# SSD exponents from log time steps, elementwise work of two stages from GpSimd to VectorE, and modulation in 256-column parts begun in the SSD stage

## The chip, the cores and the metric

The kernel runs on one core of one Trainium2 chip. TensorE (PE) multiplies matrices, VectorE (DVE), ScalarE (ACT) and GpSimd (POOL) work elementwise, SyncE (SP) issues most of the loads. The metric is the device time of one execution in microseconds: the median of three runs, 1510.19 us.

## The reference

Two layers of a diffusion backbone run over 256 context and 256 latent tokens of width 1024, with a modulation (shift, scale, gate) from a small matrix product per layer. Only what the change touches is shown. Layer 0's SSD heads are computed in chunks of 128 tokens, forward and backward:

```python
mod_l = (jax.nn.silu(c) @ ada_w[layer] + ada_b[layer])[:, None, :]       # 6 x 1024 columns
# SSD, one chunk, one direction: xi = x * dt, ai = dt * neg_a
acum = jnp.cumsum(ai, axis=-1)
seg = jnp.where(lower, acum[..., :, None] - acum[..., None, :], -jnp.inf)
scores = jnp.einsum('bgin,bgjn->bgij', ci, bi)[:, :, None] * jnp.exp(seg)
y = jnp.einsum('bgrij,bgrjp->bgrip', scores, xi)
y = y + jnp.einsum('bgin,bgrpn->bgrip', ci, h) * jnp.exp(acum)[..., None]
xw = xi * jnp.exp(acum[..., -1:] - acum)[..., None]
h = h * jnp.exp(acum[..., -1])[..., None, None] + jnp.einsum('bgjn,bgrjp->bgrpn', bi, xw)
# GLA: o from decayed q, k and v, then
o = rmsnorm(o, gla_norm_w).reshape(bn, t, GLA_VAL) * jax.nn.silu(r)
```

Then come an output projection and a squared-ReLU MLP; layer 1 has HGRN2 and S5 heads in place of SSD and GLA, and an MLP of its own.

## The kernel before, in words

Everything is in one unrolled program of 24495 instructions. Its stages follow one another: norm and the first modulation parts (0 to 45 us of the trace), layer 0's input projection with convolutions (to 155), the SSD stage (to about 313), the GLA stage (to 498), output projection, MLP 0 (600 to 975), then layer 1. The order of the instructions on each engine is made by a planner that simulates the program with a cost model of its own and takes ready work by the order of the source; engines run their queues in that order.

Weights come as 512 KB tiles into a ring of four (`wraw`, L214). Each is split on chip: `whi` is a rounded copy on ACT (L80), `wlo` the rest, a subtraction (L87) on VectorE or GpSimd, as the list `lo_eng` says in turn. Each product is three matmuls. In the SSD stage the list is `[V, G]`, in GLA `[V, V, G]`.

*Modulation* (`ada_steps`, L227 to 251): a group of 2048 columns is eight k steps and two closing steps. A k step loads two raw halves of 1024 columns into the same ring (L233) and multiplies them unsplit with 32 columns of the conditioning (L236), two matmuls of 512 columns a half, in column groups 0 and 1 for the first half, 2 and 3 for the second. The sum stays in one of the four small PSUM banks (`pss`) till the last k step. Layer 0's groups 1 and 2 are drawn by `step(ad, ...)`: `ADN` = 0, 6, 11, 0 steps in the four rounds of the GLA stage, the rest in the output projection (`WA`). Layer 1's three groups are drawn inside MLP 0. Group 0 of layer 0 is made at the start by other code (L771), with four matmuls of 256 columns per half.

*SSD stage*: `state` multiplies x with decay weights (`xw`, on GpSimd) and makes the carried states. `scan_out(c, hs)` takes a chunk: scores `Ssb`, their diagonal (`y`, on GpSimd), then four head groups of four heads. For each group two broadcasts R of cumulated decays are loaded (L975, issued on ACT's queue, one buffer each), and for 512 columns there are built X = exp(min(R0 - a0, R1 - a1)) and W = mask x (dt0 - dt1) + dt1, head by head; W is multiplied with the scores on GpSimd and X with W on VectorE, and X goes to TensorE (L998). `xtm`, the running output, is then updated by passes on VectorE and GpSimd. Between head groups `run_out` draws projection work (`fill`: `v_r_proj`, eight chunks of 256 columns with two weight tiles each).

*GLA stage*: four rounds; a round draws `fill` (the z projection), the input of the next pair of heads (`gla_in`, with `lin_elem` and `lin_states`), modulation steps, then `gla_out` for both heads of the pair: scores, masks by predicated copies (`masked`, L1172 to 1176), their sum `pa` on GpSimd, the output, and `put`, which copies it to `vtm` on ACT, squares it and multiplies it with the gate on GpSimd, sums the squares on VectorE and normalizes. `lin_out` is used by layer 1's HGRN heads too.

## Time and profile before

| | |
|---|---|
| median of three runs | 1510.19 us (1508.2 to 1517.02) |
| the profiled execution | 1509.75 us, its span 1508.0 us |
| busy: PE, PE weight loads | 1434.5 us (95%), 1220.4 us (81%) |
| busy: DVE, ACT, POOL | 965.4 us (64%), 685.5 us (45%), 490.2 us (33%) |
| moved by DMA | 222.44 MB, mean 148 GB/s |

A span is cut into stretches, and for each the busy time of every engine stands beside its length: an engine that fills its stretch sets the pace. A group line gives the number of like instructions, their busy time, the mean of one, and how long the engine stood idle before them and for whom. A mean far above the median tells that some of them were held up while they ran. `fp32` matmuls that aren't rounded appear as two records each. PE's busy time is partly modelled, so a lone matmul shows longer than it holds the engine.

### The profile page before, as it was taken

To read this page: it belongs to the slowest core of one execution; us is meant where nothing else is said; L and a number is where in the kernel's file an instruction comes from. 1 tells how busy PE (TensorE), PEld (TensorE's weight loads), DVE (VectorE), ACT (ScalarE), POOL (GpSimd) and SP (SyncE) were. 2 spreads that over 40 slices of the span, in tenths; PEclk is the share of its full clock that TensorE was granted. 3 is DMA by queue.
4 is the path that set the end of the run, shared out by engine and by line. 5 is a ranking of instruction groups with operands and counts; after the bars stand their busy time and mean duration, and the time that the engine had idled before them with its cause. 6 is when DMAs were issued, how large, how long until landed. Compare 5 with 4: busy or idle time off the path is not lost.

```text
span 1508.0 us, 24495 instructions
## 1 busy us (share of the span) xinstructions
PE 1434.5 (95%) x9598; PEld 1220.4 (81%) x9598; DVE 965.4 (64%) x1621; ACT 685.5 (45%) x1256; POOL 490.2 (33%) x454
## 2 busy tenths in 40 slices
PE   7999988789989999999999999999989999999998
PEld 4889987678845789877777777899978888899998
DVE  4798589976665445854453853373786888665553
ACT  4566345447542324531322422262376677555532
POOL 2002354534332103097066860122621120044210
PEclk9999999999999999999999999999999999999999
DMA  9632434322057443456466656648734332566762
GB/s 332 184 97 72 127 98 112 99 72 85 29 183 230 133 125 106 130 161 204 145 179 202 206 173 188 180 159 213 174 112 139 104 106 75 152 175 172 201 182 85
DMA packets 291407, 222.44 MB, mean 148 GB/s; under 512 B 22646, under 2 KB 268844, under 8 KB 291292
## 3 DMA queue, kind: packets, MB, share of 16 engines
q1 hardware_dynamic: 253584, 184.84, 42.1%
q10 hardware_dynamic: 32140, 16.09, 4.3%
q0 software_dynamic: 5568, 19.96, 4.1%
q8 instruction: 75, 1.23, 0.4%
q14 instruction: 40, 0.33, 0.1%
HBM read 206.39 MB, written 14.46 MB: 146 GB/s over the span
## 4 chain that ended last, share of the span: by engine, by line
PE 60%; DVE 15%; DMA 8%; issue 6%; POOL 5%; ACT 5%; ACTq 0%; SPq 0%; DVEq 0%; POOLq 0%
PE psd L99 52%; PE pss L99 3%; DMA R<-acd 2%; DVE wlo L87 2%; PE pss L107 2%; PE pss L236 2%; ACT whi L80 2%; DVE X L96 2%; DMA araw<-in_ada_w_dram 1%; POOL cma L87 1%; DVE ke L87 1%; POOL cmb L87 1%; DVE X L91 1%; POOL pa L87 1%; DVE hL L135 1%
## 5 line engine op out<-in xcount | busy, mean ns | idle before, releaser
L87 DVE TENSOR_TENSOR wlo<-wraw,whi 128x1024 fp32r<-128x1024 f32 (+1 forms) x225 | 301.5, 1344 | 205.8 <-ACT whi L80 194.1
L80 ACT ACTIVATE whi<-wraw 128x1024 fp32r<-128x1024 f32 (+1 forms) x250 | 260.3, 1044 | 343.7 <-DMA wraw<-in_mlp_w_dram 168.4
L99 PE MATMUL psd<-hlo,whi 128*128 128x512 f32 (+1 forms) x1112 | 383.9, 347 | 1.2 <-DVE hlo L87 1.2
L99 PE MATMUL psd<-hhi,whi 128*128 128x512 f32 (+1 forms) x1112 | 381.4, 349 | 3.4 <-ACT hhi L80 3.1
L99 PE MATMUL psd<-hhi,wlo 128*128 128x512 f32 (+1 forms) x1112 | 382.5, 346 | 1.0 <-DVE wlo L87 1.0
L99 PEld LDWEIGHTS psd<-hhi,whi 128*128 128x128 f32 x1112 | 210.9, 192 | 37.7 <-ACT mr L80 5.0
L99 PEld LDWEIGHTS psd<-hhi,wlo 128*128 128x128 f32 x1112 | 213.0, 192 | 26.0 <-DVE wlo L87 2.1
L99 PEld LDWEIGHTS psd<-hlo,whi 128*128 128x128 f32 x1112 | 212.7, 192 | 25.3 <-DVE hlo L87 1.9
L99 PE MATMUL psd<-wlo,hhi 128*128 128x256 f32 x576 | 165.4, 288 | 1.6 <-DVE wlo L87 1.6
L99 PE MATMUL psd<-whi,hlo 128*128 128x256 f32 x576 | 166.7, 290 | 0.0
L99 PE MATMUL psd<-whi,hhi 128*128 128x256 f32 x576 | 166.1, 290 | 0.0
L87 POOL TENSOR_TENSOR wlo<-wraw,whi 128x1024 fp32r<-128x1024 f32 (+1 forms) x25 | 62.2, 2489 | 243.1 <-ACT whi L80 176.2
L99 PEld LDWEIGHTS psd<-wlo,hhi 128*128 128x128 f32 x576 | 112.1, 195 | 3.2 <-DVE wlo L87 1.8
L99 PEld LDWEIGHTS psd<-whi,hlo 128*128 128x128 f32 x576 | 112.3, 195 | 1.8 <-issue 1.3
L99 PEld LDWEIGHTS psd<-whi,hhi 128*128 128x128 f32 x576 | 111.9, 195 | 1.4 <-issue 0.5
L99 PE MATMUL psd<-hidh,whi 128*128 128x512 f32 (+1 forms) x288 | 107.6, 374 | 0.0
L99 PE MATMUL psd<-hidh,wlo 128*128 128x512 f32 (+1 forms) x288 | 105.7, 367 | 0.6 <-DVE wlo L87 0.6
L99 PE MATMUL psd<-hidl,whi 128*128 128x512 f32 (+1 forms) x288 | 105.6, 367 | 0.0
L96 DVE SCALAR_TENSOR_TENSOR xtm<-psd,mod,xtm 128x256 f32<-128x256 f32 x96 | 42.3, 476 | 64.8 <-PE psd L99 57.0
L87 POOL TENSOR_TENSOR nsa<-nsa,nsq 128x256 f32<-128x256 f32 x28 | 26.2, 937 | 149.4 <-ACT nsq L80 149.1
L99 PE MATMUL psd<-hl,whi 128*128 128x256 f32 x256 | 72.9, 285 | 0.0
L99 PE MATMUL psd<-hh,wlo 128*128 128x256 f32 x256 | 72.9, 285 | 0.0
(440 smaller groups left out, 2670.7 us busy)
## 6 DMA issues: line engine op xcount, KB each, us to landing
wraw<-in_mlp_w_dram SPq DMA_DIRECT2D x128, 512.0 KB, 4.2
wraw<-in_ada_w_dram SPq DMA_DIRECT2D x80, 512.0 KB, 3.8
wraw<-in_ssd_gla_w_in_dram SPq DMA_DIRECT2D x48, 512.0 KB, 4.8
wraw<-in_hgrn_s_w_in_dram SPq DMA_DIRECT2D x43, 512.0 KB, 4.1
araw<-in_ada_w_dram SPq DMA_DIRECT2D x16, 512.0 KB, 11.6
R<-acd ACTq DMA_DIRECT2D x32, 256.0 KB, 3.6
wraw<-in_ssd_gla_w_out_dram SPq DMA_DIRECT2D x16, 512.0 KB, 4.5
wraw<-in_hgrn_s_w_out_dram SPq DMA_DIRECT2D x12, 384.0 KB, 3.2
```

Of the source, the lines that this page charges most:

```text
L80: ins = S.activation(out=out_, in_=in_, func=func, scale=scale, bias=bias)
L87: eng.tensor_tensor(out=o, in0=a, in1=b, op=op)
L91: eng.tensor_scalar(out=o, in0=a, scalar1=s1, scalar2=None, op0=op0)
L96: eng.scalar_tensor_tensor(out=o, in0=a, scalar=s, in1=b, op0=op0, op1=op1)
L99: PE.matmul(o, lhsT=l, rhs=r, start=start, stop=stop, skip_group_check=True)
L107: PE.transpose(o, i, ident[:rows, :rows])
L135: V.tensor_tensor_scan(out=o, data0=rz[:n], data1=x, initial=0.0, op0=MUL, op1=ADD)
L236: PE.matmul(ps[32 * gg:32 * gg + 32], lhsT=cs[:, k], rhs=raw[:, g * T:(g + 1) * T], start=(k == 0), stop=(k == 7), skip_group_check=True, ...
```

## The change

The SSD exponents are built from `lnd` = ln(dt) - a: for each head group R1 + lnd1 (ACT, head by head), R0 + lnd0 (VectorE, 512 columns at once), a predicated copy of the one into the other below the diagonal (mask `ms`), one exponential, one product with the scores. W and its product vanish; R gets three buffers each and X is R0 itself. The passes on GpSimd in the SSD and GLA stages and `pa` in HGRN become VectorE's, weight splits too (`lo_eng` stays `[V]` in both stages); the square of `put` is taken by ACT out of PSUM with its sum. A modulation half becomes four matmuls of 256 columns in four column groups. Modulation steps are drawn in the SSD stage as well, eight of them, and `ADN` = 2, 5, 5, 0 in GLA, which is all twenty.

```diff
-HACT = 2
-ADN = 0, 6, 11, 0
+ADN = 2, 5, 5, 0
...
-                for g in range(2):
-                    gg = 2 * hf + g
-                    PE.matmul(ps[32 * gg:32 * gg + 32], lhsT=cs[:, k], rhs=raw[:, g * T:(g + 1) * T],
-                              start=(k == 0), stop=(k == 7), skip_group_check=True,
-                              tile_position=(0, 32 * gg))
+                for g in range(4):
+                    PE.matmul(ps[32 * g:32 * g + 32, 256 * hf:256 * hf + 256], lhsT=cs[:, k],
+                              rhs=raw[:, 256 * g:256 * g + 256], start=(k + hf == 0), stop=(k + hf == 8),
+                              skip_group_check=True, tile_position=(0, 32 * g))
...
+    ms = tl(s1, [P, P], "ms")
+    asel(ms, ones, ALU.is_gt, 0.0, cm=1, pat=-1)
...
-    tt(V, ddt, dtm[:, :, 0:16], dtm[:, :, 32:48], SUB)
-    nac = tl(s1, [P, 4, 16], "nac")
-    ts(V, nac, acm[:, :, 32:48], -1.0, MUL)
+    lnd = tl(s1, [P, 4, 64], "lnd")
+    ts(V, lnd, dtm, 1e-37, MAX)
+    act(lnd, lnd, AF.Ln)
+    tt(V, lnd, lnd, acm, SUB)
...
-        tt(G, xw.rearrange("p (h d) -> p h d", h=16), xtm[:, c].rearrange("p (h d) -> p h d", h=16),
+        tt(V, xw.rearrange("p (h d) -> p h d", h=16), xtm[:, c].rearrange("p (h d) -> p h d", h=16),
...
-        tt(G, sdt, Ssb, ident.unsqueeze(1).to_broadcast([P, 4, P]), MUL)
+        tt(V, sdt, Ssb, ident.unsqueeze(1).to_broadcast([P, 4, P]), MUL)
...
-                    R.append(tl(s2, [P, 4, P], f"R{d}", bufs=1))
+                    R.append(tl(s2, [P, 4, P], f"R{d}", bufs=3))
                     S.dma_start(out=R[d], in_=acd[d, 4 * g:4 * g + 4, c * P:(c + 1) * P].partition_broadcast(P))
-                X = tl(s2, [P, 4, P], "X")
-                W_ = tl(s2, [P, 4, P], "W")
+                X = R[0]
                 for h_ in range(4):
-                    col = 4 * g + h_
-                    if h_ < HACT:
-                        act(W_[:, h_], mf, AF.Identity, scale=ddt[:, c, col:col + 1], bias=dtm[:, c, 32 + col:33 + col])
-                    else:
-                        ts(V, W_[:, h_], mf, ddt[:, c, col:col + 1], MUL, dtm[:, c, 32 + col:33 + col], ADD)
-                tt(G, W_, W_, Ssb[:, g].unsqueeze(1).to_broadcast([P, 4, P]), MUL)
-                for h_ in range(4):
-                    col = 4 * g + h_
-                    if h_ < HACT:
-                        act(X[:, h_], R[1][:, h_], AF.Identity, bias=nac[:, c, col:col + 1])
-                    else:
-                        ts(V, X[:, h_], R[1][:, h_], acm[:, c, 32 + col:33 + col], SUB)
-                    stt(V, X[:, h_], R[0][:, h_], acm[:, c, col:col + 1], X[:, h_], SUB, MIN)
+                    act(R[1][:, h_], R[1][:, h_], AF.Identity, bias=lnd[:, c, 32 + 4 * g + h_:33 + 4 * g + h_])
+                tt(V, X, X, bcol(lnd, c, 4 * g, 4, P), ADD)
+                V.copy_predicated(X, ms.bitcast(I32).unsqueeze(1).to_broadcast([P, 4, P]), R[1])
                 act(X, X, AF.Exp)
-                tt(V, X, X, W_, MUL)
+                tt(V, X, X, Ssb[:, g].unsqueeze(1).to_broadcast([P, 4, P]), MUL)
...
-            tt(G, xs3, xs3, dsk[:, 8 * hf:8 * hf + 8].unsqueeze(2).to_broadcast([P, 8, 64]), MUL)
+            tt(V, xs3, xs3, dsk[:, 8 * hf:8 * hf + 8].unsqueeze(2).to_broadcast([P, 8, 64]), MUL)
...
-                tt(G, xs, xs, t1, ADD)
+                tt(V, xs, xs, t1, ADD)
...
-    lo_eng[:] = [V, G]
     fill = v_r_proj()
...
         for i, _ in enumerate(scan_out(c, hs)):
-            if i % 2 == 1:
-                step(fill)
+            step(fill if i % 2 == 1 else ad)
...
-        tt(V if o0 else G, v3(gm), g3[:, o0:], g3[:, o0:, mid:mid + 1].to_broadcast([P, no, P]), SUB)
+        tt(V, v3(gm), g3[:, o0:], g3[:, o0:, mid:mid + 1].to_broadcast([P, no, P]), SUB)
...
-        tt(G, pa, pm[0], pm[1], ADD)
+        tt(V, pa, pm[0], pm[1], ADD)
...
-                tt(G, ys, ys, two(sg), MUL)
+                tt(V, ys, ys, two(sg), MUL)
...
-                act(ov, o3, AF.Copy)
                 sq = tl(g2, [P, 4, P], "pa", bufs=2)
-                tt(G, sq, ov, ov, MUL)
-                tt(G, ov, ov, sr[:, :, hs_], MUL)
-                V.tensor_reduce(out=osq[:, :, hd_:hd_ + 1], in_=sq, axis=mybir.AxisListType.X, op=ADD)
+                for c in range(4):
+                    S.activation(out=sq[:, c], in_=o3[:, c], func=AF.Square, accum_out=osq[:, c, hd_:hd_ + 1])
+                tt(V, ov, o3, sr[:, :, hs_], MUL)
...
-    lo_eng[:] = [V, V, G]
     cur = gla_in(0, gla_w(0))
```

## Rows read from the trace of the kernel before

**Rows 1.** Busy time by stretch: start and end, length, PE, PEld, DVE, ACT, POOL, clock, DMA.
```profile
155.00:335.00 180.00, 152.48 (x1197) 139.96 (x1196) 142.54 (x239) 81.85 (x163) 89.31 (x58) 0.94 0.38 102
200.00:313.00 113.00, 87.26 (x725) 78.53 (x723) 103.50 (x182) 54.62 (x107) 55.67 (x38) 0.94 0.40 104
335.00:424.00 89.00, 86.62 (x593) 72.92 (x592) 58.40 (x78) 57.32 (x133) 31.22 (x20) 0.99 0.17 48
424.00:498.00 74.00, 67.71 (x482) 35.99 (x479) 42.23 (x63) 22.75 (x51) 23.74 (x18) 0.96 0.73 235
600.00:975.00 375.00, 374.38 (x1917) 289.06 (x1916) 203.40 (x351) 117.22 (x160) 180.72 (x199) 1.00 0.60 177
```
**Rows 2.** Groups on VectorE, 155 to 335 us: count, busy, mean ns, idle before and releaser.
```profile
L96 DVE SCALAR_TENSOR_TENSOR X<-R,acm,X 128x128 f32<-128x128 f32 x64 | 30.6, 533 | 6.7 <-DMA R<-acd 6.7
L91 DVE TENSOR_SCALAR X<-R,acm 128x128 f32<-128x128 f32 x32 | 18.0, 601 | 6.8 <-DMA R<-acd 6.8
L87 DVE TENSOR_TENSOR wlo<-wraw,whi 128x1024 fp32r<-128x1024 f32 x11 | 17.6, 1597 | 4.0 <-ACT whi L80 3.8
L93 DVE TENSOR_SCALAR W<-mf,ddt,dtm 128x128 f32<-128x128 f32 x32 | 15.5, 527 | 0.1
L87 DVE TENSOR_TENSOR X<-X,W 128x512 f32<-128x512 f32 x16 | 12.9, 806 | 0.4 <-ACT X L80 0.3
```
**Rows 3.** Tile X on VectorE, 155 to 335 us: ns shortest/median/longest, first and last start.
```profile
L96 DVE SCALAR_TENSOR_TENSOR X<-R,acm,X x64: 334/342/2486, 166.9 to 309.5; 128x128 f32<-128x128 f32 x64
...
L87 DVE TENSOR_TENSOR X<-X,W x16: 671/680/1797, 198.3 to 310.5; 128x512 f32<-128x512 f32 x16
```
**Rows 4.** Timeline from 233 us: start, duration, engine, operation and count.
```profile
233.08 4.84 DVE L96 SCALAR_TENSOR_TENSOR X<-R,acm,X 128x128 f32<-128x128 f32 x4
...
234.00 2.46 POOL L87 TENSOR_TENSOR wlo<-wraw,whi 128x1024 fp32r<-128x1024 f32 x1
236.42 1.09 POOL L87 TENSOR_TENSOR xtm<-xtm,dsk 128x512 f32<-128x512 f32 x1
```
**Rows 5.** Load queue, 424 to 498 us: its waits (us, times, longest), its issues.
```profile
SPq L233 <- PE pss L236: 68.7, 20, 30.7
...
wraw<-in_ada_w_dram SPq DMA_DIRECT2D x26, 512.0 KB, 5.1
```
**Rows 6.** Timeline of TensorE: modulation in GLA (two halves), MLP 0, the first stage.
```profile
473.63 1.05 PE L236 MATMUL pss<-wraw,cs 128*32 128x512 f32 x4
...
475.62 1.05 PE L236 MATMUL pss<-wraw,cs 128*32 128x512 f32 x4
...
657.79 1.06 PE L236 MATMUL pss<-wraw,cs 128*32 128x512 f32 x8
...
21.32 1.93 PE L771 MATMUL pss<-araw,cs 128*32 128x256 f32 x32
```
**Rows 7.** Chain of waits, 459 to 498 us: start, us, what.
```profile
476.23 1.27 POOL vtm L87
477.50 5.23 issue
```
**Rows 8.** Durations on VectorE of near kin: ns shortest/median/longest.
```profile
L1172 DVE COPY_PREDICATED pm<-mf,pss x16: 429/576/735, 385.9 to 1274.4; 64x512 f32<-64x512 int32 x8, 64x256 f32<-64x256 int32 x8
...
L87 DVE TENSOR_TENSOR xtm<-xtm,ssqz x4: 1216/1218/1219, 402.4 to 405.8; 128x1024 f32<-128x1024 f32 x4
```
**Rows 9.** Groups on GpSimd, 155 to 335 us.
```profile
L87 POOL TENSOR_TENSOR wlo<-wraw,whi 128x1024 fp32r<-128x1024 f32 x7 | 17.2, 2453 | 17.6 <-ACT whi L80 17.6
L87 POOL TENSOR_TENSOR xtm<-xtm,y 128x512 f32<-128x512 f32 x12 | 16.6, 1383 | 22.4 <-DVE xtm L87 22.1
L87 POOL TENSOR_TENSOR xw<-xtm,wts 128x1024 f32<-128x1024 f32 x6 | 12.8, 2132 | 10.1 <-DVE wts L87 5.6 <-PE pss L99 4.4
L87 POOL TENSOR_TENSOR xtm<-xtm,dsk 128x512 f32<-128x512 f32 x8 | 8.6, 1069 | 6.2 <-DVE dsk L87 6.2
```
**Rows 10.** Groups of the whole page: projection matmuls and their wait for splits.
```profile
L99 PE MATMUL psd<-wlo,hhi 128*128 128x256 f32 x576 | 165.4, 288 | 1.6 <-DVE wlo L87 1.6
```

More of the change, by code (lines that the diff above doesn't have):

```diff
@@ L245, in ada_steps @@
             tr(p2[:, b * P:(b + 1) * P], sb[:, b * P:(b + 1) * P])
-        src = p2.rearrange("p (b g r) -> p g b r", b=4, r=32)[:, :, :, 0:2]
-        bias = vA[:, l * 48 + g3 * 16:l * 48 + g3 * 16 + 16].rearrange("p (g b) -> p g b", g=4)
-        dst = mod[l][:, g3 * 16:g3 * 16 + 16].rearrange("p (g b) s -> p g b s", g=4)
-        for s in range(2):
-            tt(V, dst[:, :, :, s], src[:, :, :, s], bias, ADD)
+        for hf in range(2):
+            o_ = g3 * 16 + 8 * hf
+            src = p2[:, 256 * hf:256 * hf + 256].rearrange("p (b g r) -> p g b r", b=2, r=32)[:, :, :, 0:2]
+            bias = vA[:, l * 48 + o_:l * 48 + o_ + 8].rearrange("p (g b) -> p g b", g=4)
+            dst = mod[l][:, o_:o_ + 8].rearrange("p (g b) s -> p g b s", g=4)
+            tt(V, dst, src, bias.unsqueeze(3).to_broadcast([P, 4, 2, 2]), ADD)
         yield
@@ L902, in emit @@
     dtm, acm, wts, eac, etot = (tl(s1, [P, 4, 64], n) for n in ("dtm", "acm", "wts", "eac", "etot"))
-    ddt = tl(s1, [P, 4, 16], "ddt")
     ps = ps_s()
```

## The prediction

> **What bounds the kernel now.** I read the busy time by stretch, then groups, timeline and waits of the slow stretches. A gain can come only where TensorE isn't dense. MLP 0 (600 to 975 us) is dense, 374.4 of 375 us. The SSD stage is not: in its core, 200 to 313 us, TensorE has 87.3 of 113 us and VectorE 103.5 [rows 1]. So VectorE sets the pace there, and the question is with what. Four groups of exponent work (X and W) take 30.6 + 18.0 + 15.5 + 12.9 = 77.0 us [rows 2]. Much of that is not work: the first of them, X of 128x128, means 533 ns, while its median is 342 and its longest 2486 [rows 3]. The timeline shows what holds the long ones: four of them take 4.84 us, from 233.08 to 237.92, while GpSimd passes of 2.46 and 1.09 us stand in a row beside them [rows 4]. A GpSimd pass here doesn't run beside VectorE's, it stops it, and the 55.7 us of GpSimd in the core [rows 1] are paid partly twice.
>
> The other hole is the end of the GLA stage, 424 to 498 us: TensorE shows 67.7 of 74 us, but only 36.0 of weight loads, and VectorE 42.2 [rows 1]. Here the modulation sets the pace. Its 26 loads of 512 KB take 5.1 us each to land, and the load queue waits 68.7 us for modulation matmuls to free weight buffers [rows 5]; half steps (x4) stand on TensorE every 2.0 us, 473.63 and 475.62 [rows 6]. TensorE runs in order, so the attention matmuls stand between them: in the chain of waits, 5.23 us of "issue" lie behind a GpSimd gate of 1.27 us and end with no visible releaser [rows 7], that is, with TensorE's queue.
>
> **The change part by part.** The sum is made against the profiled execution, 1509.75 us (span 1508.0 and 1.75 around it), 0.03% below the median 1510.19: the two are one number here.
>
> *SSD exponents and GpSimd's share, 155 to 335 us.* Removed from VectorE: the 77.0 us. Added for each of 16 head groups: a sum and a product of 512 elements, 0.68 us each (the median of the same product now [rows 3]), and a predicated copy of 512. The trace has no such copy on 128 partitions from SBUF; the nearest takes 0.735 us at most, 512 elements on 64 partitions from PSUM [rows 8]. I take 0.74; as bounds 0.43, its shortest row, and 1.4, two passes: 5 us less or 11 us more in all. So 16 x (0.68 + 0.74 + 0.68) = 33.6 us. Moved from GpSimd: 7 weight splits of 1024 elements at 1.22 us [rows 8] are 8.5; 12 and 8 passes over `xtm` at 0.68, 13.6; 6 `xw` at 1.22, 7.3 [rows 9]; 4 diagonals at 0.68, 2.7: 32.1 us. The products W x S on GpSimd vanish. VectorE's own 11 splits mean 1597 ns [rows 2] against 1.22: 4.1 us come free. VectorE in this stretch: 142.5 - 77.0 + 33.6 + 32.1 - 4.1 = 127.1 us, 15.4 less. ACT exchanges 64 small activations for 64 small ones; its 81.9 of 180 us [rows 1] hide them. The logarithm and its two small steps, 1 us, are hidden by the projection that fills TensorE at the stage's start; without it they'd cost that 1 us once. R gets three buffers for one, so the 6.7 and 6.8 us that VectorE waited for R [rows 2] are prefetched, and R's 32 loads on ACT's queue no longer wait there for the group before. What is late next is TensorE: 152.5 us busy plus eight modulation steps that come in, 8 x 1.06 [rows 6] = 8.5, is 161 of 180. So the gain lies between VectorE's 15.4 + 13.5 and TensorE's 19; I take 17, nearer to the engine that is late next. Bounds: 0 (rival 1) and 28.
>
> *Modulation begun in the SSD stage.* A group is eight k steps and two closing ones. By the counts in the code, layer 0's two groups had 15 k steps in the GLA stage and one behind it; now eight go to the SSD stage and eight stay, with both closings. The 16 loads (8.4 MB) that SP issues earlier enter a stretch that moves 102 GB/s, against 235 in the tail [rows 1]: bandwidth hides them. But they share four weight buffers with the projection's loads, stand ahead of these in SP's queue, and their sum holds one of four small PSUM banks all through. In the tail, 7 steps fewer are 14 loads at 2.0 us [rows 6], 28 us. Late next is the last head pair's chain: mask copies, `pa`, the output. Its GpSimd passes (the gate 1.27 us [rows 7], `pa` and the square like it) become 0.68 us on VectorE and squares on ACT straight from PSUM, about 2 us less for each of the tail's heads. I take 27 for the tail, 74 to 47 us; bounds 4 (the chain is as long as the tail was) and 40 (no load is waited for).
>
> *The form of the modulation.* Before, a half alone (x4, two column groups) costs the same 1.05 us as a whole step (x8, four groups) with 1.06. In four 256-column groups 32 records take 1.93 us in the first stage [rows 6], 0.06 each against 0.13; a whole step will have 16, 0.97 us. So where both halves have landed, as in MLP 0, nothing changes: 24 x (0.97 - 1.06) is 2 us less; I take 0, bounds 2 less and 5 more. Lone halves gain some 0.5 us each, and these lie within the tail's 27.
>
> *GLA's front, 335 to 424 us.* TensorE 86.6 of 89 us [rows 1]. Splits, `gm`, `pa` and gates go to VectorE, 58.4 busy; half of GpSimd's 31.2 is 16 and fits. I take 4, for shorter chains; bounds 4 more, and 8 on the other side if splits come late.
>
> *The rest.* One k step and the closings leave the output projection, which is dense: 1.5 us. In HGRN eight `pa` move to VectorE: 0, bounds 3 either way.
>
> Sum: 17 + 27 + 0 + 4 + 1.5 = 49.5, so 1460 us.
>
> **A rule against the change.** The trace has 256-column tiled matmuls at half the time of 512-column ones, 0.06 and 0.13 us a record [rows 6]. The Trainium skill, page "TensorEngine Tiling (Array Packing)", section Performance Considerations, says that each matmul carries about 60 cycles of overhead. By that page twice the instructions would cost, as an estimate, 8 x 25 ns x 24 steps = 5 us in MLP 0, and the sum would come to 1465; the trace speaks against it, since the first stage's 0.06 us a record has whatever overhead there is within it. Rival 3 below is the like mechanism priced from rows, with a chance of its own.
>
> **The rivals.**
> 1. *The SSD stage gives nothing back.* The eight steps share the ring of four weight buffers and hold a small PSUM bank, so the projection's loads and the products with the carried states come late. For: the load queue waited 68.7 us for just such steps [rows 5]. Against: the stretch moves only 102 GB/s. Price 17: 1477.
> 2. *The tail keeps its length*, bound by the last pair's chain and not by loads. For: VectorE has 42.2 of 74 us, so latency may rule. Against: the even 2.0 us spacing. 23 of 27 stay: 1483.
> 3. *A 256-column tiled record costs what a 512-column one does*: 8 x 0.13 x 24 = 25 us in MLP 0, 1485. Against: the first stage's 0.06 us.
> 4. *Both 1 and 2*: 1460 + 17 + 23 = 1500 to 1506, hardly to be told from no change.
> 5. *Slower: weight splits queue on VectorE.* By the code 32 splits of projection weights in the SSD and GLA stages now all stand in VectorE's order behind the elementwise work. If each makes TensorE wait 2.0 us (three 0.68 us passes ahead of it), that is 64 us: 1524. It decides from 1.55 us a split, where 49.5 is eaten. For: VectorE was full in the core. Against: it gets 15 us lighter, and this projection's matmuls waited 1.6 us for VectorE's splits in the whole run [rows 10].
>
> **How the numbers follow.** The forecast (both gains, 1440 to 1475) has 0.60; rival 1 0.17; rival 2 0.08; rival 3 0.04; rival 4 0.05; rival 5 0.06. The predicted time is the likeliest case's, 1460. The range: below, 1460 less 11 (SSD) and 13 (tail) and 2 (MLP 0), 1434; above, rivals 1 to 3 and the 5 and 8 us of the small bounds on them, 1494. A measurement of this kernel tells about 0.5%, 7.5 us, from no change. Faster is the forecast and rivals 1 to 3, 0.89; same is rival 4, 0.05; slower is rival 5, 0.06.
>
> **What would show it.** Right: VectorE's X groups at their undisturbed 0.68 us, none of 2 us in the SSD stage; no wait for R; the SSD stage's last X product some 17 us earlier; the first output projection 42 to 48 us earlier; eight modulation steps before 300 us; an MLP 0 as long as before. Wrong: TensorE waiting for `wlo` (rival 5), TensorE idle ahead of modulation steps in the SSD stage (rival 1), an unchanged distance from the last keys' projection to the output projection (rival 2), modulation steps of 1.9 us in MLP 0 (rival 3).

## The result: slower, 1530 us, and the profile after

| | before | after |
|---|---|---|
| median, us | 1510.31 | 1530.05 |
| span of the profiled execution, us | 1508.0 | 1525.8 |
| last X product of the SSD stage (end), us | 313.4 | 308.0 |
| last keys' projection evicted (end of the GLA front), us | 419.3 | 424.6 |
| first transpose of the output projection (end of the GLA tail), us | 491.2 | 512.5 |
| last hidden tile of MLP 0, us | 946.1 | 967.0 |

The changed kernel takes 1.0136 times as long as the one before, 95% interval 1.0113 to 1.0159. The prediction was 1460. All medians here and below are of fast runs, without those over 1.5% above the same kernel's fastest: that leaves out one of the four runs of e1 (with it 1492.7, which later expectations name) and five of the ten of e3 (with them 1517.5). From MLP 0 on, everything is late by 15 to 22 us, so the loss lies ahead of it: the SSD stage gained 5 us where 17 were forecast, the GLA front gave these back and 5 more, and the GLA tail, where 27 us were to be won, grew by 16 (71.9 to 87.9 us between the last keys' projection and the first transpose).

The busy time by stretch, columns as in [rows 1]: the whole SSD part, the GLA front, the GLA tail and MLP 0, with the last two moved along with the work.

```profile
155.00:335.00 180.00, 154.23 (x1291) 135.25 (x1289) 122.78 (x184) 80.72 (x163) 0.98 (x2) 0.94 0.52 147
335.00:424.00 89.00, 87.70 (x603) 74.82 (x599) 61.57 (x90) 55.34 (x142) 0.00 (x0) 1.00 0.21 60
424.00:513.00 89.00, 76.55 (x490) 50.89 (x490) 44.46 (x74) 26.97 (x91) 0.00 (x0) 0.58 0.40 119
620.00:995.00 375.00, 373.97 (x2093) 293.64 (x2092) 201.44 (x350) 116.65 (x160) 182.26 (x198) 1.00 0.60 176
```

VectorE did what was forecast: 122.8 us in 155 to 335 for 142.5 (127.1 predicted). TensorE has as much work as before there. What is new is the granted clock of the tail, 0.58 for 0.96. Its two levels are 1.2 and 2.4 GHz; here TensorE ran at the lower one most of the time.

The groups of VectorE in the same 155 to 335 us answer [rows 2] and [rows 3]:

```profile
L86 DVE TENSOR_TENSOR wlo<-wraw,whi 128x1024 fp32r<-128x1024 f32 x19 | 23.2, 1220 | 12.9 <-ACT whi L79 12.9
L982 DVE COPY_PREDICATED R<-ms,R 128x512 f32<-128x512 int32 x16 | 11.5, 735 | 0.0
L86 DVE TENSOR_TENSOR R<-R,lnd 128x512 f32<-128x512 f32 x16 | 10.9, 688 | 19.6 <-DMA R<-acd 19.6
L86 DVE TENSOR_TENSOR R<-R,Ssb 128x512 f32<-128x512 f32 x16 | 10.3, 683 | 0.1
```

The three passes of the exponents take 11.5 + 10.9 + 10.3 = 32.7 us, where 33.6 were predicted and 77.0 removed; the predicated copy takes 0.735 us (0.74 predicted), and splits are back at 1220 ns. So the part of the sum that was worked out most carefully came true to a microsecond, and the time went the other way. One sign failed in the same rows: VectorE waits 19.6 us for the loads of R, and not less than the 13.5 us of before [rows 2], though R has three buffers now.

Where it went, first place. The load queue (SP) from 100 to 260 us; L232 loads modulation weights, L213 projection weights:

```profile
106.86 5.78 SPq L232 DMA_DIRECT2D wraw<-in_ada_w_dram  x2
117.74 6.28 SPq L213 DMA_DIRECT2D wraw<-in_ssd_gla_w_in_dram  x2
130.00 6.24 SPq L232 DMA_DIRECT2D wraw<-in_ada_w_dram  x2
191.73 1.23 SPq L213 DMA_DIRECT2D wraw<-in_ssd_gla_w_in_dram  x2
195.99 3.01 SPq L232 DMA_DIRECT2D wraw<-in_ada_w_dram  x2
```

The raw tiles of the first two modulation steps, four loads, have gone out by 136 us and hold all four buffers. Then this queue loads nothing for 55 us, and the next load goes out at 191.73. TensorE in that time, without the projection matmuls:

```profile
171.84 3.78 PE L98 MATMUL pss<-xw,btm 128*128 128x256 f32 x8 [7.20 <-DVE xw L86]
178.89 3.46 PE L98 MATMUL pss<-xw,btm 128*128 128x256 f32 x8 [3.27 <-ACT R L79]
184.36 1.97 PE L98 MATMUL pss<-xw,btm 128*128 128x256 f32 x8 [2.01 <-DVE xw L86]
...
190.59 1.93 PE L234 MATMUL pss<-wraw,cs 128*32 128x256 f32 x16
```

The first modulation step runs at 190.59, and a microsecond later the queue goes on. In between TensorE waits for `xw` (7.20 and 2.01 us) and for ScalarE's R behind it (3.27), with no projection work to put there, since its weights aren't loaded. Busy time by stretch, after:

```profile
150.00:175.00 25.00, 15.62 (x99) 13.72 (x98) 11.05 (x18) 10.14 (x29) 0.00 (x0) 0.88 0.37 88
175.00:200.00 25.00, 16.36 (x127) 10.97 (x126) 15.47 (x23) 6.76 (x15) 0.00 (x0) 0.85 0.33 95
```

and before:

```profile
150.00:175.00 25.00, 24.94 (x197) 24.02 (x196) 14.80 (x30) 8.74 (x19) 6.25 (x3) 1.00 0.48 139
175.00:200.00 25.00, 24.87 (x193) 23.90 (x194) 15.08 (x17) 9.20 (x15) 16.12 (x8) 1.00 0.34 97
```

TensorE has 32.0 of 50 us, before 49.8. The projection that filled these holes comes later, so VectorE's 20 us are not turned into time.

Second place, the tail. TensorE's timeline from 436 us:

```profile
436.81 1.08 PE L234 MATMUL pss<-wraw,cs 128*32 128x256 f32 x8 [3.31 <-DMA wraw<-in_ada_w_dram]
...
473.03 0.90 PE L106 MATMUL pss<-ident,ke 128*128 128x128 f32 x3 [5.38 <-DVE ke L86]
...
492.77 1.75 PE L98 MATMUL pss<-g0qt,g0kt 64*64 64x128 f32 x15
...
496.01 0.79 PE L98 MATMUL pss<-vtm,pa 128*128 128x128 f32 x2
...
502.65 1.75 PE L98 MATMUL pss<-g0qt,g0kt 64*64 64x128 f32 x15
```

TensorE stands idle for 3.31 us for a modulation load, and the half step behind it takes 1.08 us (0.64 at full clock). The clock comes back once, behind 32 modulation records in a row (460.33 to 463.97 us): at 467.02 a half step takes 0.64 us again. Then TensorE idles for 5.38 us, for `ke`, and from there to 519 us every duration is that of the low clock. One head's outputs (from its first `vtm,pa` pair to the next head's scores) take 496.01 to 502.65, 6.64 us. The like work of a head before, at full clock, with two half steps of the modulation (L236) in it:

```profile
483.39 1.08 PE L99 MATMUL pss<-g0qt,g0kt 64*64 64x128 f32 x16
484.40 1.05 PE L236 MATMUL pss<-wraw,cs 128*32 128x512 f32 x4
...
486.40 1.05 PE L236 MATMUL pss<-wraw,cs 128*32 128x512 f32 x4
487.39 0.49 PE L99 MATMUL pss<-vtm,pa 128*128 128x128 f32 x2
...
491.17 1.09 PE L107 MATMUL pss<-ident,xtm 128*128 128x128 f32 x8
```

Its outputs take 487.39 to 491.17, 3.78 us. With its scores a head takes 9.9 us (492.77 to 502.65), before 5.8 (483.39 to 491.17 less the two half steps, 2.0). TensorE is busy without a break from 478.9 to 519.8 us with such matmuls; 40.8 us at 5.8/9.9 would be 24, so by this estimate the clock costs some 17 us there. Of the 40.8 us, 33.6 lie ahead of the first transpose, where the tail as measured here ends; in them it is some 14 of the 16 us by which the tail grew.

### The profile page after: what moved, and what is told of

Its sections match the earlier page's. It is cut to its first block, busy times and chain, and to the rows that moved or that the text cites. A ratio compares the mean times of both kernels' runs of the same rounds, so it can differ in the third digit from the quotient of the medians.

```text
span 1525.8 us, 24985 instructions
## 1 busy us (share of the span) xinstructions
PE 1450.6 (95%) x9918; PEld 1241.9 (81%) x9918; DVE 944.9 (62%) x1600; ACT 685.1 (45%) x1313; POOL 331.1 (22%) x348
## 4 chain that ended last, share of the span: by engine, by line
PE 72%; DVE 11%; DMA 10%; ACT 4%; issue 2%; ACTq 1%; SPq 0%; DVEq 0%
PE psd L98 59%; PE pss L98 7%; DMA R<-acd 4%; PE pss L234 2%; DVE wlo L86 2%; PE pss L106 2%; DMA wraw<-in_ssd_gla_w_in_dram 2%; DMA araw<-in_ada_w_dram 1%; DVE hL L134 1%; ACT whi L79 1%; ACT hL L79 1%; DMA wraw<-in_mlp_w_dram 1%; DVE ke L86 1%; DMA wraw<-in_ada_w_dram 1%; DVE xtm L86 0%
## 5 line engine op out<-in xcount | busy, mean ns | idle before, releaser
L86 DVE TENSOR_TENSOR wlo<-wraw,whi 128x1024 fp32r<-128x1024 f32 (+1 forms) x238 | 306.3, 1290 | 220.8 <-ACT whi L79 218.9
L98 PE MATMUL psd<-whi,hlo 128*128 128x256 f32 x576 | 163.4, 284 | 0.0
L98 PE MATMUL psd<-hh,whi 128*128 128x256 f32 x256 | 72.4, 283 | 0.0
## 6 DMA issues: line engine op xcount, KB each, us to landing
araw<-in_ada_w_dram SPq DMA_DIRECT2D x16, 512.0 KB, 11.5
```

The source lines that it names most:

```text
L86: eng.tensor_tensor(out=o, in0=a, in1=b, op=op)
L98: PE.matmul(o, lhsT=l, rhs=r, start=start, stop=stop, skip_group_check=True)
```

## The experiments

Two theories stood from these traces. *Ring and clock*: the early modulation steps take all four weight buffers and starve the projection, and the thinned GLA tail loses TensorE's clock; the exponents are a gain that both hide. The rivals: the passes moved to VectorE eat what the exponents give; or the 256-column form is to blame. The table gives all runs; "tail" is the time from the last keys' projection to the first transpose of the output projection, "clock" the granted clock in that time. Ratios are against the kernel before, on the same chip; a ratio comes from the runs and isn't quite the quotient of two medians. All columns but the median and the ratio are read from one execution each.

| kernel | median us | ratio (95%) | last X product | last keys | tail us | clock |
|---|---|---|---|---|---|---|
| before | 1510.3 | 1 | 313.4 | 419.3 | 71.9 | 0.95 |
| after | 1530.1 | 1.0136 (1.0113 to 1.0159) | 308.0 | 424.6 | 87.9 | 0.58 |
| e1 after, steps late | 1488.6 | 0.9865 (0.9791 to 0.9938) | 283.3 | 390.8 | 96.6 | 0.61 |
| e2 before, steps early | 1531.2 | 1.0152 (1.0094 to 1.0209) | 326.9 | 441.1 | 74.1 | 0.73 |
| e3 after, first two steps ahead | 1504.3 | 0.9996 (0.9954 to 1.0039) | 306.3 | 422.9 | 74.9 | 0.69 |
| e4 after, dense filler | 1534.3 | 1.0157 (1.0102 to 1.0213) | 312.8 | 471.0 | 53.8 | 0.87 |
| e5 e1 with the old form | 1480.5 | 0.9789 (0.9735 to 0.9842) | 285.1 | 392.3 | 79.7 | 0.87 |
| e6 before, new form | 1513.2 | 1.0031 (1.0007 to 1.0055) | 314.2 | 420.0 | 77.1 | 0.78 |
| e7 before, exponents alone | 1488.7 | 0.9849 (0.9803 to 0.9895) | 280.5 | 397.2 | 71.9 | 0.93 |
| e8 e1, mixer early | 1489.4 | 0.9847 (0.9791 to 0.9902) | 283.1 | 390.6 | moved | |
| e9 e5, mixer early | 1483.4 | 0.9846 (0.9796 to 0.9896) | 282.1 | 388.8 | moved | |
| e10 e1, records twice | 1498.6 | 0.9937 (0.991 to 0.9964) | 281.5 | 388.3 | 91.7 | 0.85 |
| e11 e7, mixer early | 1490.1 | 0.9879 (0.9848 to 0.9911) | 282.1 | 398.8 | moved | |
| e12 e5, GLA passes on GpSimd | 1478.1 | 0.9812 (0.9794 to 0.9831) | 282.7 | 392.3 | 71.5 | 1.00 |

### The place of the modulation steps (e1, e2, e3)

**e1**, the changed kernel with the steps where they stood:

```diff
-ADN = 2, 5, 5, 0
+ADN = 0, 6, 11, 0
-            step(fill if i % 2 == 1 else ad)
+            if i % 2 == 1:
+                step(fill)
```

> The changed kernel, but with the modulation's eight k steps of the SSD stage put back to where the kernel before had them (none in the SSD stage, 6 and 11 in the GLA stage). Exponents, GpSimd's share and the 256-column form stay as changed. Theory (the early steps starve the projection of weight buffers, and leave the GLA tail too thin for TensorE's clock): both losses go, the gains of the exponents show, 1480 to 1497 us; last X product 295 to 303 us (308.0 in the changed kernel, 313.4 before), granted clock over 0.9 from 475 to 525 us, first transpose of the output projection before 485 us (512.5 and 491.2). Rival A (the passes moved from GpSimd to VectorE cost what the exponents gain): 1508 to 1530, X products as in the changed kernel. Rival B (the 256-column form costs in MLP 0 or the tail): 1510 to 1525 with the SSD stage short and the tail or MLP 0 long.

1488.6 us: within the theory's range, and the SSD stage ends 30 us before that of the kernel before. Rival A is out. The clock, though, did not come back: in the execution traced the tail is the longest of all, 96.6 us, with the kernel before's placement of the steps. So early steps cost the front 34 us (424.6 against 390.8), and something else in the change costs the clock.

**e2**, the kernel before with the opposite edit of the same lines.

> The kernel before with one part of the change alone: the modulation's eight k steps begun in the SSD stage (2, 5, 5 in the GLA stage), in their old form of 512 columns. Theory: this part alone loses what the whole change loses and more, since nothing offsets it: 1530 to 1555 us, a stretch of over 40 us without a projection load after the second pair of modulation steps is loaded, and a granted clock near 0.5 at the end of the GLA stage. Rival A (VectorE's new load is the loss): within 10 us of before, 1500 to 1520. Rival C (the loss comes only of early steps together with the shorter form, because half as much work stands in the tail): SSD hole as in the theory, clock of the tail above 0.8, 1515 to 1530.

1531.2 us, as the theory said, and the same hole in the load queue (L233 modulation, L214 projection): from 138 to 196.71 us, ended by the first modulation step at 194.74.

```profile
131.88 5.97 SPq L233 DMA_DIRECT2D wraw<-in_ada_w_dram  x2
196.71 0.93 SPq L214 DMA_DIRECT2D wraw<-in_ssd_gla_w_in_dram  x2
```

```profile
194.74 1.94 PE L236 MATMUL pss<-wraw,cs 128*32 128x512 f32 x8
```

Rival A is out here too. Its tail by stretch:

```profile
441.00:475.00 34.00, 28.43 (x203) 13.22 (x202) 19.75 (x28) 12.26 (x33) 11.17 (x8) 0.96 0.71 230
475.00:515.00 40.00, 37.02 (x220) 28.69 (x219) 19.57 (x34) 10.13 (x22) 8.24 (x7) 0.54 0.25 69
```

The tail keeps its clock as long as modulation steps last (0.96; the last one ends at 474.7 us) and loses it behind them (0.54), in the old form too. So it isn't shorter for the steps that left it: 74.1 us for 71.9. Rival C, a clock above 0.8, is out (0.73).

**e3** takes the first two steps out of the scan of the first chunk and puts them ahead of it:

```diff
     step(fill)
+    step(ad, 2)
     def run_out(c, hs):
...
-            step(fill if i % 2 == 1 else ad)
+            if i % 2 == 1:
+                step(fill)
+            elif c:
+                step(ad)
```

> The changed kernel with the first two modulation steps issued ahead of the scan of the first chunk (behind the first projection step), not inside it; the other six of the SSD stage stay. Theory: what starves the projection is that the raw tiles of these two steps hold all four weight buffers from 118 to 191 us while TensorE reaches their matmuls only behind the first X products; issued ahead, they are used when they land, loads go on between 136 and 190 us, the first silu of the second projection comes at about 205 us (247.5 in the changed kernel, 200.2 before) and the SSD stage with the GLA front gains 10 to 17 us. The tail stays at the low clock: 1510 to 1520 us. If the sum's PSUM bank or VectorE is the cause, the gap between 136 and 190 us may go but the last X product stays at 308 us, 1525 to 1535.

The load queue, and TensorE's first two steps:

```profile
107.99 17.11 SPq L232 DMA_DIRECT2D wraw<-in_ada_w_dram  x4
174.95 2.39 SPq L213 DMA_DIRECT2D wraw<-in_ssd_gla_w_in_dram  x4
```

```profile
174.25 1.93 PE L234 MATMUL pss<-wraw,cs 128*32 128x256 f32 x32
```

Half a hit. The steps ran at 174.25 us instead of 190.59, and the queue's hole ended with them, at 174.95 instead of 191.73: it is the held buffers that stop the loads, and they are free when the steps have run. But TensorE took them only behind the first two products with `xw`, for the second of which it had idled 6.88 us; so 50 us of hole remained, the second projection's first silu came at 245.6 us (205 expected, 247.5 in the changed kernel), and the front gained 2 us. The whole kernel comes out level with the kernel before, by a tail that is 13 us shorter (clock 0.69 for 0.58) though nothing was changed in it; the tail's clock is touchy, and this kernel's times spread from 1495.8 to 1516.1 us. The steps ran without a wait of their own when TensorE came to them, so it was their place in its order that held them; whether the planner put them there for the PSUM bank of their sum was not told apart. A ring of their own for the modulation's raw tiles, which would be the plain proof, found no room beside the SSD stage's tiles and wasn't tried.

### The form and the clock (e5, e6, e4, e10)

**e5** is e1 with the old form (two column groups of 512 per half). What is left are the exponents and the moves off GpSimd.

```diff
-                for g in range(4):
-                    PE.matmul(ps[32 * g:32 * g + 32, 256 * hf:256 * hf + 256], lhsT=cs[:, k],
-                              rhs=raw[:, 256 * g:256 * g + 256], start=(k + hf == 0), stop=(k + hf == 8),
+                for g in range(2):
+                    gg = 2 * hf + g
+                    PE.matmul(ps[32 * gg:32 * gg + 32], lhsT=cs[:, k], rhs=raw[:, g * T:(g + 1) * T],
+                              start=(k == 0), stop=(k == 7), skip_group_check=True,
```

> The changed kernel without either edit of the modulation: no early steps, and the form of 512 columns in two column groups per half, as before. What is left of the change are the exponents and the moves off GpSimd. Theory (in the thin GLA tail a lone half in four 256-column groups occupies TensorE for 0.6 us instead of 1.05, the engine idles for the next load, its clock falls to 1.2 GHz and the small attention matmuls then run at half speed): the granted clock of the tail returns to over 0.9, the way from the last keys' projection to the first transpose of the output projection goes from 96.6 us (with the late steps in the new form) to 70 to 76 us, and the kernel takes 1465 to 1475 us. Rival (the tail is slow because its passes left GpSimd, so that VectorE's chain got longer or TensorE waits for it): the clock stays near 0.5 to 0.6 and the time at 1488 to 1497.

1480.5 us: 8 less than e1, clock 0.87 for 0.61, tail 79.7 for 96.6. The direction is the theory's; the time is 5.5 us above its range, the tail 4 to 10 us longer than expected, and e12 below finds what was missing. The whole times of e1 and e5 alone don't settle it, since their intervals overlap. TensorE's busy time in the tail, for e1, e5 and (below) e12, tells that it is neither waits nor work:

```profile
391.00:487.00 96.00, 86.72 (x598) 51.31 (x596) 41.54 (x69) 25.11 (x82) 0.00 (x0) 0.61 0.56 177
```

```profile
392.00:472.00 80.00, 69.61 (x480) 36.12 (x479) 40.06 (x68) 23.06 (x80) 0.00 (x0) 0.87 0.59 194
```

```profile
392.00:464.00 72.00, 64.02 (x481) 33.10 (x482) 39.28 (x62) 22.45 (x54) 19.23 (x15) 1.00 0.67 220
```

Idle time of TensorE is 9.3, 10.4 and 8.0 us, about the same in all. Its busy time falls from 86.7 to 69.6 to 64.0 us as the granted clock rises from 0.61 to 0.87 to 1.00, though e1's tail has the least modulation work when priced at full clock (0.64 us a half for 1.05).

**e6** is the kernel before with the new form alone (the reverse of e5's edit).

> The kernel before with the form of the modulation alone changed to four 256-column groups; the steps stand where they stood. Theory: the SSD stage and MLP 0 stay within 3 us, the GLA tail falls to the low clock and gets 12 to 25 us longer: 1520 to 1535 us. Rival (the form is free and the clock falls for the moves off GpSimd or for the shorter stage ahead of it): 1500 to 1512 us with a granted clock above 0.9 from 425 to 500 us.

1513.2 us, ratio 1.0031, just clear of the noise: the mechanism is there (clock 0.78, tail longer by 5 us), but at less than half the expected price, and the time is near the rival's range. It isn't a matter of one execution: the mean clock of the whole kernel is 0.971 to 0.976 in all ten runs, and 0.974 to 0.984 in the thirteen of the kernel before beside them. The clock recovers to 0.97 from 475 to 500 us there. Why the form costs more in e1, beside the other edits, was not shown.

**e4**, the changed kernel with 16 dense matmuls for each of six heads, whose sums nobody reads:

```diff
+DENSE = 16
...
+        if n == 4 and dense:
+            d_ = ps_d()
+            for j in range(dense[0]):
+                i_ = PE.matmul(d_, lhsT=h[0][:, j % 8, 0:P], rhs=h[0][:, j % 8], start=True, stop=True,
+                               skip_group_check=True)
+                behind(i_, last[0])
```

> The changed kernel plus work whose sums nobody reads: 16 dense 128x128 by 512-column matmuls for each of the last six GLA heads, behind the head's last score matmul, some 22 us of TensorE work at 2.4 GHz (16 x 6 x 0.23 us). Theory (TensorE's clock falls to 1.2 GHz in the thin tail and stays there until the dense projection): the granted clock from 450 to 525 us rises from 0.50 to 0.57 to over 0.8, and although work is added the first transpose of the output projection comes no later than 512 us: 1515 to 1530 us. If the clock isn't held by the density of work, or the tail is bound by its chain of small steps whatever the clock, the added work costs 10 to 22 us: 1540 to 1552.

Stretches of its tail:

```profile
450.00:475.00 25.00, 23.29 (x152) 16.95 (x144) 8.02 (x13) 7.56 (x26) 0.00 (x0) 1.00 0.20 66
...
500.00:525.00 25.00, 25.00 (x182) 19.37 (x179) 12.71 (x21) 4.88 (x30) 0.00 (x0) 1.00 0.01 1
```

The clock did rise where the filler stood (1.00 in 450 to 475 and 500 to 525, 0.73 between; 0.57, 0.52 and 0.50 in the changed kernel), and of some 22 us of added work 12 came out at the first transpose (524.8 for 512.5). But the filler also pushed the last keys' projection to 471.0 us, so it weighs less than expected: 1534.3 us, above the theory's range by 4 and below the rival's by 6.

**e10**, e1 with each record of layer 0's two groups issued twice and the sums halved:

```diff
-                for g in range(4):
+                for g in range(4 if l else 8):
+                    j, g = g, g % 4
...
-        act(sb, ps, AF.Copy)
+        act(sb, ps, AF.Copy, scale=1.0 if l else 0.5)
```

> The changed kernel with the late modulation steps in the new form, but in layer 0's two groups each 256-column record issued twice and the sums halved: twice the TensorE work for the modulation in the GLA tail, the same loads. Nothing but TensorE's occupancy differs from the kernel with late steps (1492.7 us, 96.6 us from the last keys' projection to the first transpose of the output projection). Theory (TensorE's clock falls because a half in the new form leaves the engine idle until the next load): the clock of the tail rises from 0.53 to 0.70 towards 0.8 to 1.0, the tail falls to 75 to 86 us, and the kernel takes 1474 to 1486 us, less time for more work. Rival (the clock isn't it; the new form's tail is long for its number of records or for its waits): 34 halves of 0.6 us more on TensorE, 1500 to 1515 us.

1498.6 us, neither the theory's 1474 to 1486 nor quite the rival's. Its tail by stretch, and TensorE's timeline, say why:

```profile
388.00:428.00 40.00, 33.31 (x394) 18.92 (x394) 20.53 (x35) 14.86 (x49) 0.00 (x0) 0.97 0.64 211
428.00:458.00 30.00, 27.17 (x341) 16.25 (x341) 7.38 (x16) 4.56 (x11) 0.00 (x0) 0.92 0.72 225
458.00:492.00 34.00, 31.70 (x146) 25.26 (x147) 19.26 (x28) 11.22 (x47) 0.00 (x0) 0.55 0.29 82
```

```profile
417.87 0.49 PE L98 MATMUL pss<-vtm,pa 128*128 128x128 f32 x2
...
460.30 1.75 PE L98 MATMUL pss<-g0qt,g0kt 64*64 64x128 f32 x15 [3.58 <-DVE vtm L86]
...
463.54 0.79 PE L98 MATMUL pss<-vtm,pa 128*128 128x128 f32 x2
...
470.18 1.75 PE L98 MATMUL pss<-g0qt,g0kt 64*64 64x128 f32 x15
```

While modulation steps stand between the heads the clock is 0.97 and 0.92, and a head's outputs from 417.87 on go by at 0.38 to 0.49 us a pair. At full clock the steps are through sooner, at 455 us. Then TensorE idles 3.58 us for `vtm`, the clock falls to 0.55 for the last heads, and the same outputs take 0.63 to 0.79 us a pair, 6.64 us in all (463.54 to 470.18). So the extra work did hold the clock, but only as long as it lasted; what it gave, the last heads took back.

The runs of one and the same kernel tell the clock's price apart from every edit. e1's three took 1496.8, 1488.6 and 1478.7 us with a mean clock of 0.968, 0.973 and 0.980: span times clock is 1447 us in all three. e10's nine go from 1503.6 us at 0.976 to 1493.4 at 0.984, the product within 2 us of 1466. So what differs between such runs is the clock, and e1's trace, of the slowest of the three, shows its tail at the long end.

### Exponents, moves, and dense work in the tail (e7, e12, e8, e9, e11)

**e7** is the kernel before with the exponents alone: all GpSimd passes and splits, the old form and the late steps as before.

> The kernel before with the exponents of the SSD stage alone changed (logarithms, three buffers for R); the passes on GpSimd, the weight splits there, and the modulation stay as before. It splits the 30 us that the SSD stage gained when both were changed. If GpSimd's passes stretch VectorE's (the 0.68 us pass beside a GpSimd pass of the same length takes twice as long), the exponents alone give 10 to 20 us: last X product 293 to 303 us, 1488 to 1500 us in all, and the moves give the rest. If the moves are neutral (what GpSimd does comes back on VectorE), the exponents give the whole 27 to 32 us: last X product 281 to 287 us, 1470 to 1482 us.

1488.7 us, within the first case; but the stage's end, 280.5 us, is that of the second. The exponents alone shorten the SSD stage by 33 us, of which 22 are left at the end of the GLA front, where TensorE is dense and has projection to catch up with (570 of its matmuls in the trace for 511 before). VectorE's passes in 155 to 335 us:

```profile
L86 DVE TENSOR_TENSOR R<-R,Ssb 128x512 f32<-128x512 f32 x16 | 17.2, 1101 | 5.6 <-ACT Ssb L79 5.6
L982 DVE COPY_PREDICATED R<-ms,R 128x512 f32<-128x512 int32 x16 | 16.9, 1063 | 4.1 <-ACT R L79 4.0
L86 DVE TENSOR_TENSOR R<-R,lnd 128x512 f32<-128x512 f32 x16 | 14.8, 928 | 6.2 <-DMA R<-acd 6.2
```

49 us with GpSimd's passes beside them, 33 without: the stretching that [rows 4] showed is real. The Trainium skill, page "SBUF — State Buffer", section Terms, says that VectorE and GpSimd share one port pair, held for a whole instruction while the other blocks; these means (928 to 1101 ns for 683 to 735) agree with that.

**e12** is e5 with the GLA stage's share of GpSimd left as it was (`gm`, `pa` with HGRN's, the gate product, the output's square and gate, a third of the splits); only the SSD stage's moves stay.

```diff
-        tt(V, pa, pm[0], pm[1], ADD)
+        tt(G, pa, pm[0], pm[1], ADD)
...
-                for c in range(4):
-                    S.activation(out=sq[:, c], in_=o3[:, c], func=AF.Square, accum_out=osq[:, c, hd_:hd_ + 1])
-                tt(V, ov, o3, sr[:, :, hs_], MUL)
+                tt(G, sq, ov, ov, MUL)
+                tt(G, ov, ov, sr[:, :, hs_], MUL)
+                V.tensor_reduce(out=osq[:, :, hd_:hd_ + 1], in_=sq, axis=mybir.AxisListType.X, op=ADD)
```

> The exponents and the SSD stage's moves off GpSimd, late modulation steps in the old form (1480.5 us with all moves), and the GLA stage's passes (the gate products, the mask sum, the output's square and gate, a third of the weight splits) left on GpSimd as before. With all moves the way from the last keys' projection to the first transpose of the output projection took 79.7 us, with none 71.9; the last keys' projection stood at 392.3 and 397.2 us. If the moves in the GLA stage make its tail longer (VectorE's passes stand in one row), the tail comes back to 71 to 74 us with the last keys' projection between 390 and 396 us: 1472 to 1479 us. If the difference is the clock's (0.80 and 0.80 against 0.80 and 1.00 in the two windows) and not the moves', the tail stays between 76 and 82 us and the time at 1478 to 1486 us.

1478.1 us, tail 71.5 us with the clock at 1.00 throughout, last keys at 392.3 us: the first case in all three numbers. It is faster than both kernels, 0.9812 of the one before (0.9794 to 0.9831). Against e7 the moves of the SSD stage give 5 us at the last keys' projection, and against e5 those of the GLA stage lengthen the tail by 8 (in the whole, 1480.5 and 1478.1 us, the two can't be told apart); of the 8, by the stretches under e5, 5.6 are TensorE's slower matmuls (69.6 us busy for 64.0, clock 0.87 for 1.00) and 2.4 its idle time. Why the clock fell with these moves wasn't shown.

**e8, e9, e11** put real dense work into the tail: the transposes of the SSD result and the first eight products of the output projection, ahead of the last head pair's attention instead of behind it, in e1, e5 and e7.

```diff
             drain(fill)
             step(ad, max(0, 10 - adn[0]))
+            mixer(0, xtm, range(8))
         gla_out(t_, cur)
...
-    for part, src in enumerate((xtm, vtm)):
+    mixer(1, vtm, range(4))
```

> The changed kernel with the late modulation steps (new form), and the first half of the output projection (the transposes of the SSD result and its eight products, all of it work that has to be done anyway) issued ahead of the last GLA head pair's attention instead of behind it. It puts dense matmuls into the thin tail. Theory: granted clock over 0.85 on average from 440 us to the end of the stage, and the whole kernel 1462 to 1480 us (the late steps alone gave 1492.7). Rival (the tail is bound by its own chain and by the modulation's loads, whatever the clock): 1488 to 1500 us, since the same work only changes places.

> The exponents and the moves off GpSimd, late modulation steps in the old form of 512 columns (1480.5 us as measured), and the first half of the output projection issued ahead of the last GLA head pair's attention. If the tail is still lengthened by the low clock (0.80 from 400 to 450 us there), dense work in it gives 5 to 15 us: 1465 to 1476 us. If it only changes places, as with the new form (1489 against 1493 us), 1476 to 1484 us.

> The kernel before with the exponents alone changed (1488.7 us as measured), and the first half of the output projection issued ahead of the last GLA head pair's attention. Its tail is already at a clock of 0.80, then 1.00, and as long as before, 71.9 us. If what is left of the tail is bound by loads of the modulation and its chain, the dense work hides some of it, 3 to 10 us: 1478 to 1486 us; if TensorE's sum of work binds, nothing: 1486 to 1492 us.

1489.4, 1483.4 and 1490.1 us, against 1488.6, 1480.5 and 1488.7 without: nothing that can be told. MLP 0's first hidden tile comes 6 us sooner in e8, and 2 and 10 us later in e9 and e11. In e8 the clock is low ahead of the moved work (0.52 from 400 to 425 us) and again behind it (0.69 from 525 to 550), where the last heads' attention now stands nearly alone. The low stretch is moved, not removed.

## Why the prediction was wrong

The five parts of the change, each as the difference between two kernels that differ in it (medians set against the kernel before of their own series: e7 1507.3, e12 1506.4, e5 1507.3, e1 1506.4, after 1510.3). By the intervals above each is good to some 7 to 14 us: the first and the last are clear of the noise; of the three between, whole times alone show nothing, and what is said of them rests on the traces and, for the form, on e6:

| step | us |
|---|---|
| exponents: before to e7 | -18.6 |
| SSD moves off GpSimd: e7 to e12 | -9.7 |
| GLA moves off GpSimd: e12 to e5 | +1.5 |
| new form: e5 to e1 | +9.1 |
| early steps: e1 to after | +37.5 |
| sum: before to after | +19.7 |

1. *SSD exponents and GpSimd's share*, -17 predicted. The costs were right (32.7 us for 33.6), and the gain was taken too low: both parts together give 28 us. The 17 lay outside the two bounds that the step named, 19 and 15.4 + 13.5, and 28 is near the upper one. The step took TensorE's 19 us as the next limit, counting the early modulation steps into its work. Without these TensorE gets denser in the stage (170 of 180 us in e12, 152 before), and the time comes from its idle time. The 13.5 us of waits for R in the upper bound were not what went: e1, e5 and e12 still have 13.4 to 15.8.
2. *Modulation begun in the SSD stage* is the step that failed, and in both halves. In the SSD stage it named the mechanism, four weight buffers shared, and rival 1 gave it 0.17 at a price of 17, the gain of that stage alone. That was no bound: measured it is some 37 us, for a starved projection also empties the holes that it had filled, so TensorE idles 18 us more in 150 to 200 us, and the front ends 34 us later than with late steps. Evidence against it was read from bandwidth (102 GB/s), and bandwidth wasn't the resource (in the hole the core moved 54 GB/s); the load queue's order and the time until TensorE reaches the step were, and that was there to be read: the first step was placed behind the first head group, whose X x W product [rows 3] put at 198 us. The sign named for this rival, TensorE idle ahead of modulation steps, wasn't the one that showed: it idled for `xw`, with the projection missing that used to hide it.
3. *The tail*, -27 predicted, +16 measured. The step took 2.0 us a load as the pace and let 28 us of loads go. It left out that these loads' matmuls held TensorE's clock while attention matmuls ran between them: in e2, where nothing but the steps' place is changed, the tail gets 2 us longer, and heads without steps between them go at the low clock. A head then costs 9.9 us for 5.8. Within the bundle the +16 has three parts, by one trace each: the moves off GpSimd in GLA 8 (71.5 to 79.7 us, e12 to e5), the form 17 (to 96.6, e1), the early steps -9 (to 87.9). So the loads that left did give 9 of 28 us where the clock was lost already. No rival held this: rival 2 kept the tail's length, none made it longer, though [rows 1] shows how thin weight loads are there (36.0 of 74 us).
4. *The form of the modulation*, 0 predicted with 2 less and 5 more as bounds. In MLP 0 that held: a whole step takes 1.07 us for 1.06 (0.97 predicted), and MLP 0 is as long as before. But a lone half's 0.64 us instead of 1.05 was booked as a gain within the tail's 27, and was a loss: 5 us by itself (e6), in the tail of the bundle 17 by the trace of e1's slowest run: less work between two loads, a lower clock.
5. *GLA's front*, -4 predicted. By the moves alone it is about 2 less (107 us from the last X product to the last keys with them, 110 without, e5 and e12), and both end at 392.3 us.
6. *Rival 5*, splits on VectorE, priced at 64 us, didn't come. TensorE's waits for `wlo` sum to 1.9 us in the whole run (3.2 before), and e5, with all splits on VectorE and 7.0 us of such waits, is 2% faster than before. Rival 3 didn't come either: 16 records of 256 columns take 1.07 us in MLP 0, 0.07 each for 0.13; nor is the 5 us of the rule weighed against the change to be seen there.

The forecast's sign and its 0.89 rested on steps 2 and 3 costing nothing beyond their own gains. Slower stood at 0.06, with a mechanism that had no part in it. The range's upper end, 1494, doesn't come out of the terms that it names either: rival 3's 1485 with the 5 and 8 us would be 1498; the measured time is far above both.

## What to carry to other kernels

Before a load is moved ahead, look for the moment at which its consumer runs, not for free bandwidth: until then it holds its buffer, and in a ring shared with other loads it holds theirs. And work that looks like filler between small matmuls may be what keeps TensorE's clock up: where a stretch has little but small matmuls, price it at both clocks before anything is taken out of it. Change one thing of a bundle at a time: here a gain of 28 us was hidden by losses of some 9 and 37.

## What the runs showed of the hardware

```profile
475.00:500.00 25.00, 24.54 (x154) 19.57 (x154) 13.86 (x27) 5.34 (x20) 0.00 (x0) 0.50 0.26 72
500.00:525.00 25.00, 25.00 (x106) 19.99 (x106) 10.14 (x16) 7.35 (x34) 0.00 (x0) 0.52 0.00 0
525.00:550.00 25.00, 25.00 (x120) 20.79 (x119) 11.29 (x17) 6.90 (x8) 0.00 (x0) 1.00 0.46 149
```

In the changed kernel TensorE is busy 24.5 and 25.0 of 25 us from 475 to 525 us, with attention matmuls back to back, and the granted clock stays at 0.50 and 0.52. It rises only after 519.76 us, with the dense 512-column projection, and is 1.00 from 525 on. Falls stand behind idle stretches of 3.31 and 5.38 us here, and 3.58 us in e10, but of 1.85 us only in e2, where the same four matmuls then go from 0.44 to 0.69 us, and of 1.26 us in the kernel before (421.30 to 421.95 us, 0.44 to 0.70):

```profile
477.72 0.44 PE L99 MATMUL pss<-vtm,g1kd 128*64 128x128 f32 x4 [1.85 <-ACT g1kd L80]
...
479.29 0.69 PE L99 MATMUL pss<-vtm,g1kd 128*64 128x128 f32 x4 [0.47 <-ACT su L80]
```

The Trainium skill, page "TensorE: Matmul & The Clock Gate", section "HAM oscillation — how this bites in real kernels", tells of falls behind waits for loads. The row of 3.31 us agrees; the others stand behind waits for VectorE and ScalarE. That TensorE can be busy for 40 us without a gap and stay at the lower level is what the rows add; what these matmuls lack can't be read from the runs.

The price of the lower clock differs by the matmul, as the rows give durations. A pair of 128x128 output products takes 0.79 for 0.49 us, sixteen 64-column score products 1.97 for 1.09, a half step of the modulation 1.08 for 0.64.
